# Mixer's room in two pools, the first down pair's weights beside the output projection, pinned forms in the second pass, loads in turns

## The chip, the cores and the metric

The kernel runs on 1 core of one Trainium2 chip. The metric is the device time of one execution in microseconds, taken as the median of several runs. The profile comes from one execution of its own.

## The reference, cut to what matters

Two layers of a decoder trunk on x of 256 rows and 2048 columns, all in float32:

```
for l in range(2):
    h    = rmsnorm(x, attn_norm_g[l])
    proj = h @ w_in[l]                    # 2048 x 6144: q | k | v | gate_b | gate_c | conv_in
    attn = diff_attention(norm(q), norm(k), v)     # 8 heads, T5 bias, difference of two softmaxes
    conv = gate_b * causal_conv3(gate_c * conv_in)
    x    = x + concat([rmsnorm(attn) * c, conv]) @ w_out[l]     # 2048 x 2048
    x    = x + relu(rmsnorm(x) @ w_up[l])**2 @ w_down[l]        # 2048 x 8192 x 2048
```

## The kernel before, in words

**Products.** Every float32 product is made of three products of rounded parts (TERMS): each operand is split into a high part, rounded by ACT, and a low part, the remainder, made by DVE. So each weight tile costs one load (issued on SP's queue), one ACT operation (`whi`, `uhi`, `b1h` and the like) and one DVE operation (`wlo`, `ulo`, `b1l`). The class Weights holds such jobs in a list; `take()` gives the next one to the matmuls and makes up to three more ahead (AHEAD).

**Order.** PE's instructions run in the order in which they are traced. For the other engines, a scheduler with a simulated timeline chooses the order at compile time; an engine then runs its list strictly in that order. The helper `late` pins an instruction behind the one traced before it on its engine. `Background` pieces are generators; `work.tick()`, called between matmuls, moves each of them on, so transpositions, norms and attention are laid between the matmuls of the projections.

**Mixer.** x stands in four chunks of 512 columns. At the start `first_loads` loads x and the first weights, and `Norm.chunk` transposes a chunk on PE (eight 128x128 pieces, `tpn`), splits it with the gain (`split_gained`, ACT L255 and DVE L256) and squares it for the norm (ACT L437). The squares are pinned. Chunk 0's loads alternate with the halves of the first weight (`cut`). Thirteen small tensors (gains, taps, lambdas, the bias table) are loaded on POOL's queue. Then `linear` makes q, k and v of four heads, again for the other four, then the conv's parts (`gc`, `ci`, `gb`), then the output projection `o`, four columns of 22 us. Biases, q, k, v, conv and the concatenated result share one pool, `bpool`, with eight buffers of 8 KB a partition.

**MLP, first pass.** The hidden width is cut into 32 blocks of 256. For block i, PE makes two columns of the up product (`up`, `upw`, `upc`, L856), ACT and DVE evict, apply ReLU (L873), scale (L875) and square (L877), and `rounded` splits the result into f (L893, L894), stored to DRAM by POOL (`plain`, `hid`). Two blocks behind it (LAG), 30 of the blocks multiply with w_down's left half by a Strassen-like scheme of seven products (L902) in place of eight. Its weight forms are made by `quarters`: `b1`, `b2` from the raw rows (`draw`), `t13` and `t24` from sums `t` (L754, L757, L758), each split by L740 (ACT) and L741 (DVE). One such set is called a pair here. `b2`, `t` and `t13` have one buffer, `b1` and `t24` two, `draw` three. The first pair is made by `begin`, called after block 0's square, and pinned. The last two blocks (30 and 31) multiply plainly (L982).

**MLP, second pass.** For w_down's right half the blocks come back: the plain ones from `plain` in pairs called `block(b)` (`g`, loaded on POOL's queue), 24 matmuls each (L1061); the twelve in SEVEN = 4, 6, 8, 11, ... from `hid` with the seven products (21 matmuls, L902, `rt`). `made_in` orders where the weights are made: `slots` lays the four jobs of a SEVEN block (plain, sums, its f, more) between those of the plain blocks before it.

**Pools.** Pools are laid one after another and a later pool waits for the tiles that lie under it. In the MLP `upool` (24 KB) and `fpool` (24 KB) lie under `dpool` (24 KB) and `spool` (48 KB).

Of the kernel before, what the change touches and what calls it, by code (L numbers as in the profile page):

```python
# [9 lines left out]
F32 = mybir.dt.float32  # L10
# [92 lines left out]
def trunk(ctx: ExitStack, tc: tile.TileContext, x, w_in, w_out, conv_w, q_norm_g, k_norm_g,  # L103
# [30 lines left out]
    def load_x(n, lo=0, hi=CH):  # L134
        nc.sync.dma_start(
            xs[n][:, :, lo:hi],
            x[0, :, n * CH + lo:n * CH + hi].rearrange("(t p) c -> p t c", p=P))
# [6 lines left out]
    nc.vector.memset(ones, 1.0)  # L144
    warm = bank("warm")
# [16 lines left out]
    ngains = const.tile([P, NG], F32, tag="ngains", name="ngains")  # L162
# [12 lines left out]
    nc.gpsimd.dma_start(vec[0:NCW, :], conv_w.rearrange("l i (k p) -> (l i k) p", p=P))  # L175
    for i, g in enumerate((q_norm_g, k_norm_g)):
        for m in range(2):
            nc.gpsimd.dma_start(
                vec[QG + i * DEPTH:QG + (i + 1) * DEPTH, m * DK:(m + 1) * DK], g)
    nc.gpsimd.dma_start(vec[QG + 2 * DEPTH:MG, :], subln_g)  # L180
    nc.gpsimd.dma_start(vec[MG:ROWS, :], mlp_norm_g.rearrange("l (k p) -> (l k) p", p=P))
    lamv = const.tile([1, 4, DEPTH, DK], F32, tag="lamv", name="lamv")
    for i, a in enumerate((lambda_q1, lambda_q2, lambda_k1, lambda_k2)):
        nc.gpsimd.dma_start(lamv[:, i], a[None])
    sel = const.tile([NB + 1, REL], F32, tag="sel", name="sel")
    nc.gpsimd.dma_start(sel, selector)
    rel = const.tile([NB + 1, 2 * NH], F32, tag="rel", name="rel")
    nc.vector.memset(rel[NB:NB + 1, :], NEG)
    nc.gpsimd.dma_start(rel[0:NB, :], rel_bias)
# [44 lines left out]
    def load_bias(l, bpool, bias):  # L234

        if l == 0:
            yield from small_setup()
        revs = []
        for j in range(2):
            rev = bpool.tile([P, NH, S], F32, tag="b", name=f"rev{l}{j}")  # L240
# [12 lines left out]
    def split_gained(dst, k, src, gain):  # L253

        nc.scalar.activation(dst[:, 0, k], src, AF.Copy, scale=gain)  # L255
        nc.vector.scalar_tensor_tensor(  # L256
            dst[:, 1, k], src, gain, dst[:, 0, k].bitcast(F32), op0=ALU.mult, op1=ALU.subtract)
# [15 lines left out]
    class Weights:  # L273
# [9 lines left out]
        def halves(self, raw, c=slice(None)):  # L283

            i = len(self.made)
            shape = [P] + list(raw.shape[1:])
            hi = wpool.tile(shape, F32R, tag="hi", name="whi")
            lo = wpool.tile(shape, F32R, tag="lo", name="wlo")
            first = self.cut and i < 2
            for k in (slice(0, 1), slice(1, None)) if first else (slice(None),):  # L290
                a = nc.scalar.activation(hi[:, k], raw[:, k], AF.Copy)  # L291
                d = nc.vector.tensor_sub(lo[:, k], raw[:, k], hi[:, k].bitcast(F32))  # L292
                if first:
                    late(a)
                    late(d)
            return hi, lo

        cut = False

        def plain(self, w, row, c, nk):  # L300
# [7 lines left out]
            def load():  # L308
                raw = self.pool.tile([P, nk, cols], F32, tag="raw", name="raw", bufs=RAW)
                src = w[row:row + nk * P, c:c + cols].rearrange("(k p) c -> p k c", p=P)  # L310
                if self.cut and not self.made and not self.early:
                    for k in range(nk):
                        load_x(0, k * CH // 2, (k + 1) * CH // 2)
                        nc.sync.dma_start(raw[:, k], src[:, k])
                else:
                    nc.sync.dma_start(raw, src)
# [10 lines left out]
        def take(self):  # L327
# [4 lines left out]
            ahead = min(max(i - 1, 0), AHEAD) if self.cut else AHEAD  # L332
# [5 lines left out]
            return self.made.pop(i) if not self.cut else self.made[i]  # L338
# [69 lines left out]
    class Norm:  # L408
# [3 lines left out]
        def __init__(self, which, l):  # L412
            self.which, self.l = which, l
            self.tiles = [Parts(apool, "a", f"nT{which}{l}_{n}") for n in range(D // CH)]
            self.ss = small.tile([P, NT, D // CH], F32, tag="ss", name=f"ss{which}{l}", bufs=2)

        def chunk(self, n, wait, banks=None):
            yield wait
            a = self.tiles[n].open()
            for j in range(2):  # L420
# [12 lines left out]
                if j == 0 and n == 0 and (self.which, self.l) == (0, 0):  # L433
                    yield 1
# [6 lines left out]

        def factors(self):
            while not all(t.ready == KG for t in self.tiles):
                yield 1
# [179 lines left out]
    def mixer(l, norm, loads):  # L624

        with ExitStack() as scope:
# [3 lines left out]
            bpool = scope.enter_context(tc.tile_pool(name="bpool", bufs=8))  # L630
            weights = Weights(rpool)
            weights.cut = l == 0
# [13 lines left out]
            work.start(load_bias(l, bpool, bias), 10)  # L646
            hT = norm.tiles
            cat = [Parts(bpool, "b", f"cat{l}{i}") for i in range(4)]
            work.start(norm.factors(), 1)
            for half in range(2):  # L650
# [3 lines left out]
                qT = bpool.tile([P, 2, 4, S], F32R, tag="b", name=f"qT{l}{half}")  # L654
                work.start(qk_norm(acc, r, qT, q_gain[:, l:l + 1], f"q{l}{half}"))
                acc = linear(f"k{l}{half}", hT, weights)
                kT = bpool.tile([P, 2, 4, S], F32R, tag="b", name=f"kT{l}{half}")
                work.start(qk_norm(acc, r, kT, k_gain[:, l:l + 1], f"k{l}{half}"))
                acc = linear(f"v{l}{half}", hT, weights)
                v = bpool.tile([P, 2, NT, CH], F32R, tag="b", name=f"v{l}{half}")  # L660
# [7 lines left out]
            cv = bpool.tile([P, AW // P, S], F32, tag="b", name=f"cv{l}")  # L668
# [24 lines left out]
    def mlp(l, mnorm, last):  # L693
# [3 lines left out]
        with ExitStack() as scope:  # L697
            upool = scope.enter_context(tc.tile_pool(name="upool", bufs=3))
            fpool = scope.enter_context(tc.tile_pool(name="fpool", bufs=2))
            dpool = scope.enter_context(tc.tile_pool(name="dpool", bufs=3))  # L700
            spool = scope.enter_context(tc.tile_pool(name="spool", bufs=1))
# [22 lines left out]
            def load_rows(i, col):  # L724
                raw = (upool.tile([P, 2, 2 * CH], F32, tag="uraw", name="raw") if col and i not in SEVEN else
                       dpool.tile([P, 2, 2 * CH], F32, tag="draw", name="draw"))
# [5 lines left out]
            def quarters(i, col=0):  # L732


                keep = late if i == 0 and col == 0 else lambda ins: None

                def parts(src, tag, bufs):
                    hi = spool.tile(list(src.shape), F32R, tag=f"{tag}h", name=f"{tag}h", bufs=bufs)
                    lo = spool.tile(list(src.shape), F32R, tag=f"{tag}l", name=f"{tag}l", bufs=bufs)
# [10 lines left out]
                def sums():  # L750
                    raw = forms["raw"]
                    t = forms["t"] = spool.tile([P, 4, CH], F32, tag="t", name="t")
# [51 lines left out]
            def load_again(i):  # L804
                again[i] = fpool.tile([P, 8, P], F32, tag="h", name="h", bufs=2)
# [24 lines left out]
            for i in SEVEN:  # L830
                before = [j for j in mine if j < where[i]][-4:]
# [37 lines left out]
            def square(i, h):  # L869
# [18 lines left out]
                nc.gpsimd.dma_start(plain[b // 2][:, b % 2], f[:, :, :4])  # L888
# [8 lines left out]
            prods = {}  # L897
# [8 lines left out]
            for i in range(NP):  # L906
                j = i - LAG
                end = i == NP - 1
                h = fpool.tile([P, 8, P], F32, tag="h", name="h", bufs=2)
                if i == 0:  # L910
# [8 lines left out]
                    forms["begin"]()  # L919
# [85 lines left out]
            for i in range(NP):  # L1005
# [29 lines left out]
                if slot == 0 and b == 0:  # L1035
                    block(1)
# [33 lines left out]
    def first_loads(weights):  # L1070
        for n in range(1, D // CH):
            weights.load_early(2)
            load_x(n)
            work.start(norm.chunk(n, 2), 4 * n - 2)
        work.start(norm.chunk(0, 0))
        work.tick()
        warm_up(5)
# [36 lines left out]
```

## Time and profile before

| what | us |
|---|---|
| median of 3 runs | 2163.86 (2161.31 to 2164.84) |
| the profiled execution | 2163.51 |
| its span, first to last instruction | 2161.7 |
| mean granted TensorE clock | 0.996 |
| DVE busy | 1692.1 |
| ACT busy | 1301.1 |

Times in rows are microseconds from the start of the span. In a row of the waits stand the engine and line, what it waited for, then the total, the number of times and the longest. In a row of the timeline stand start, duration, engine, line, operation, tiles, shapes and count, and in brackets the idle time before it with what ended that. In a row of the chain of waits stand start, duration and what. In a row of a window stand its two ends, its length, the busy time and instruction count of PE, PEld, DVE, ACT and POOL, then the granted clock, the DMA share and GB/s. In a row of the groups, "x84 | 102.4, 1219" is the count, the busy time in us and the mean in ns.

### The profile page before, as it was taken

The numbers are of one execution on the slowest core, as the hardware profiler recorded it, in microseconds if no ns is written. First come the engines' busy times: TensorE is split into PE (matmuls) and PEld (weight loads), VectorE is DVE, ScalarE is ACT, GpSimd is POOL, SyncE is SP. The second block draws the span as 40 slices with busy tenths as digits, with TensorE's granted clock in tenths as the row PEclk, the third lists the DMA queues.
The fourth block names the chain that finished last, engine by engine and source line by source line (L and its number), as shares of the span: only waits on it lengthen the run. The fifth ranks groups of instructions, "written<-read, shape, count | busy, mean of one in ns | idle before, by whom it ended". The sixth has DMA issues, their size and how long they took to land.

```text
span 2161.7 us, 29004 instructions
## 1 busy us (share of the span) xinstructions
PE 2136.9 (99%) x10966; PEld 1815.0 (84%) x10966; DVE 1692.1 (78%) x2301; ACT 1301.1 (60%) x1760; POOL 176.1 (8%) x266
## 2 busy tenths in 40 slices
PE   9999999999999999999999999999999999998999
PEld 7888888788888888788888888888888888887887
DVE  5677655699888888889766776557988888887796
ACT  6556445576666667556565654446766666665563
POOL 3021200000000000100001222000000000001000
PEclk9999999999999999999999999999999999999999
DMA  7555766587777777888456557656877777779882
GB/s 256 177 165 162 240 186 189 175 260 237 230 229 226 231 233 229 298 302 301 165 171 180 159 165 244 186 165 217 259 231 225 231 234 225 227 231 304 308 299 77
DMA packets 288413, 477.05 MB, mean 221 GB/s; under 512 B 10931, under 2 KB 191749, under 8 KB 288272
## 3 DMA queue, kind: packets, MB, share of 16 engines
q1 hardware_dynamic: 268128, 417.89, 61.8%
q0 software_dynamic: 20096, 57.28, 7.8%
q8 instruction: 86, 1.41, 0.3%
q14 instruction: 55, 0.45, 0.1%
q10 hardware_dynamic: 48, 0.02, 0.0%
HBM read 441.04 MB, written 34.10 MB: 220 GB/s over the span
## 4 chain that ended last, share of the span: by engine, by line
PE 92%; DVE 3%; DMA 2%; issue 2%; POOL 1%; ACT 1%; DVEq 0%; POOLq 0%; ACTq 0%
PE upc L856 30%; PE pr L902 13%; PE rt L1061 10%; PE o L361 8%; PE rt L902 5%; PE ci L383 4%; PE gc L383 4%; PE gb L383 4%; PE v L361 4%; PE q L361 3%; PE k L361 3%; DMA draw<-in_w_down_dram 1%; PE up L856 1%; PE pr L982 1%; DVE ulo L720 1%
## 5 line engine op out<-in xcount | busy, mean ns | idle before, releaser
L292 DVE TENSOR_TENSOR wlo<-raw,whi 128x1024 fp32r<-128x1024 f32 (+1 forms) x338 | 414.6, 1229 | 273.7 <-ACT whi L291 267.8
L291 ACT ACTIVATE whi<-raw 128x1024 fp32r<-128x1024 f32 (+1 forms) x338 | 356.0, 1055 | 437.6 <-PE rt L1061 120.5
L856 PE MATMUL upc<-nT,uhi 128*128 128x512 f32 x1920 | 477.6, 391 | 0.0
L719 ACT ACTIVATE uhi<-uraw 128x1024 fp32r<-128x1024 f32 x256 | 270.4, 1056 | 262.8 <-PE upc L856 228.0
L856 PEld LDWEIGHTS upc<-nT,uhi 128*128 128x128 f32 x1920 | 352.7, 188 | 68.3
L720 DVE TENSOR_TENSOR ulo<-uraw,uhi 128x1024 fp32r<-128x1024 f32 x256 | 313.0, 1223 | 115.2 <-ACT uhi L719 104.8
L856 PEld LDWEIGHTS upc<-nT,ulo 128*128 128x128 f32 x1920 | 261.9, 190 | 18.7
L856 PE MATMUL upc<-nT,ulo 128*128 128x256 f32 x1920 | 267.7, 282 | 0.0
L1061 PE MATMUL rt<-whi,g 128*128 128x512 f32 x608 | 191.9, 389 | 0.0
L361 PE MATMUL o<-whi,cat 128*128 128x512 f32 x512 | 159.6, 390 | 0.0
L1061 PEld LDWEIGHTS rt<-whi,g 128*128 128x128 f32 x608 | 114.1, 188 | 23.6
L1061 PE MATMUL rt<-wlo,g 128*128 128x512 f32 x304 | 118.3, 389 | 0.0
L361 PEld LDWEIGHTS o<-whi,cat 128*128 128x128 f32 x512 | 96.1, 188 | 19.8
L741 DVE TENSOR_TENSOR t13l<-t,t13h 128x1024 fp32r<-128x1024 f32 x84 | 102.8, 1223 | 3.1
L741 DVE TENSOR_TENSOR b2l<-draw,b2h 128x1024 fp32r<-128x1024 f32 x84 | 102.3, 1218 | 1.1 <-ACT b2h L740 1.1
L754 DVE TENSOR_TENSOR t<-draw 128x1024 f32<-128x1024 f32 x84 | 102.3, 1218 | 0.6 <-DMA draw<-in_w_down_dram 0.6
L741 DVE TENSOR_TENSOR t24l<-t,t24h 128x1024 fp32r<-128x1024 f32 x84 | 102.4, 1219 | 0.2
L361 PE MATMUL o<-wlo,cat 128*128 128x512 f32 x256 | 99.6, 389 | 0.0
L894 DVE TENSOR_TENSOR f<-h,f 128x896 fp32r<-128x896 f32 (+2 forms) x88 | 98.7, 1121 | 0.2
L902 PE MATMUL pr<-t13h,f 128*128 128x512 f32 x240 | 93.8, 391 | 0.0
L740 ACT ACTIVATE t13h<-t 128x1024 fp32r<-128x1024 f32 x84 | 89.4, 1064 | 6.4 <-PE rt L902 2.4
L740 ACT ACTIVATE b2h<-draw 128x1024 fp32r<-128x1024 f32 x84 | 88.4, 1052 | 6.4 <-PE pr L902 3.8
(359 smaller groups left out, 3831.9 us busy)
## 6 DMA issues: line engine op xcount, KB each, us to landing
uraw<-in_w_up_dram SPq DMA_DIRECT2D x128, 1024.0 KB, 5.9
raw<-in_w_in_dram SPq DMA_DIRECT2D x191, 512.0 KB, 4.0
draw<-in_w_down_dram SPq DMA_DIRECT2D x88, 1024.0 KB, 5.9
raw<-in_w_down_dram SPq DMA_DIRECT2D x40, 1024.0 KB, 6.4
raw<-in_w_out_dram SPq DMA_DIRECT2D x64, 512.0 KB, 3.7
plain<-f POOLq DMA_DIRECT2D x40, 512.0 KB, 3.8
g<-plain POOLq DMA_DIRECT2D x40, 512.0 KB, 9.6
hid<-h POOLq DMA_DIRECT2D x24, 448.0 KB, 6.1
```

The costliest lines, as they stand in the source:

```text
L291: a = nc.scalar.activation(hi[:, k], raw[:, k], AF.Copy)
L292: d = nc.vector.tensor_sub(lo[:, k], raw[:, k], hi[:, k].bitcast(F32))
L361: nc.tensor.matmul(acc[:, t], a.ap[:, pa, k % KG, t * P:(t + 1) * P], (hi, lo)[pw][:, j], start=(k == 0 and n == 0), stop=(k == nk - 1 and ...
L383: nc.tensor.matmul(acc[:, f, 0] if part else acc[:, f], wt[:, k % 4, fs], a.ap[:, 0, k % KG] if part else a.ap[:, :, k % KG], start=(part ...
L719: nc.scalar.activation(hi, src, AF.Copy)
L720: nc.vector.tensor_sub(lo, src, hi.bitcast(F32))
L740: keep(nc.scalar.activation(hi, src, AF.Copy))
L741: keep(nc.vector.tensor_sub(lo, src, hi.bitcast(F32)))
L754: keep(nc.vector.tensor_sub(t[:, 0:2], raw[:, :, 1], raw[:, 0]))
L856: nc.tensor.matmul(acc[:, 0] if part else acc, wt[:, k], a.ap[:, 0, k % KG] if part else a.ap[:, :, k % KG], start=(part == 0 and kh == 0 ...
L902: nc.tensor.matmul(prods[n], f[:, pa, a], b[pw], start=(start and m == 0), stop=(stop and m == 2))
L1061: nc.tensor.matmul(prods[p], blocks[b][:, slot, pa, 2 * k + t], w[pw][:, n], start=(i == PLAIN[0] and k == 0 and m == 0), stop=False)
```

## The change

Five edits:

- The start. `Norm.begin` replaces the chunks of the first norm: eight steps, each of four transpositions and then, in turn for two columns k, the split of x (ACT, DVE) and half a weight (ACT, DVE), all pinned. The squares come in behind the sixth step and later. x's first half chunk is the first load, the second half goes on ACT's queue; a one-column copy on ACT comes early; the small loads move from POOL's queue to SP's, pinned behind the loads of x; three warm-up matmuls stand where five stood.
- The mixer's pool of eight buffers becomes two pools of four single-buffer tags: `cats` (the four concatenated tiles, and before them q, k, v of the first half) and `spare` (bias tables, q, k, v of the second half, conv).
- In the MLP `second` and `first` replace `dpool` and `spool`; `tile_of` gives each tile its room by turns. `upool` (24 KB), `fpool` (20 KB), `second` (32 KB), `first` (44 KB): `second` lies on the room of `cats`, `first` on that of `spare`. The first pair is made entirely where the jobs are listed, ahead of the up product in the trace, and is not pinned.
- In the second pass the forms of the first SEVEN block (4) are pinned, and its jobs stand behind weights 0, 1, 5 and 3 instead of 4 to 7.
- `block(1)` is issued on POOL behind the last store of `plain`.

```diff
+    load_x(0, 0, CH // 2)
     nc.scalar.dma_start(ngv, attn_norm_g.rearrange("l (k p) -> (l k) p", p=P))
+    load_x(0, CH // 2, CH, nc.scalar)
+    nc.scalar.activation(ngains[:, :1], ones[:, :1], AF.Copy)
...
+    def small_loads():
+        def load(dst, src):
+            late(nc.sync.dma_start(dst, src))
...
+        def in_turns(self, split):
+            j = self.traced
+            self.traced += 1
+            raw = self.early.pop(0) if self.early else self.jobs[j].load()
+            hi, lo = self.made[j] = self.pair(raw)
+            for k in range(2):
+                split(k)
+                late(nc.scalar.activation(hi[:, k], raw[:, k], AF.Copy))
+                late(nc.vector.tensor_sub(lo[:, k], raw[:, k], hi[:, k].bitcast(F32)))
...
+        def begin(self, weights):
+            at = 0
+            for j, step in enumerate((0, 1, 3, 4, 6, 8, 10, 12)):
+                if step > at:
+                    yield step - at
+                    at = step
...
+                if j == 0:
+                    warm_up(3)
+                weights.in_turns(lambda i: split_gained(...))
+                if j >= 5:
+                    self.squares(j - 5)
+            yield 1
+            self.squares(3)
...
-            bpool = scope.enter_context(tc.tile_pool(name="bpool", bufs=8))
+            cats = scope.enter_context(tc.tile_pool(name="cats", bufs=1))
+            spare = scope.enter_context(tc.tile_pool(name="spare", bufs=1))
...
-            dpool = scope.enter_context(tc.tile_pool(name="dpool", bufs=3))
-            spool = scope.enter_context(tc.tile_pool(name="spool", bufs=1))
+            second = scope.enter_context(tc.tile_pool(name="second", bufs=1))
+            first = scope.enter_context(tc.tile_pool(name="first", bufs=1))
+            def tile_of(tag, shape, dtype, *rooms):
+                n = turn[tag] = turn.get(tag, -1) + 1
+                pool, tag_in = rooms[max(n - (tag == "draw"), 0) % len(rooms)]
+                return pool.tile(shape, dtype, tag=tag_in, name=tag, bufs=1)
...
-                keep = late if i == 0 and col == 0 else lambda ins: None
+                keep = late if i == SEVEN[0] and col else lambda ins: None
...
                 if i == 0 and col == 0:
-                    made = {}
-                    begin = lambda: made.update(p=plain(), s=sums())
-                    forms["begin"] = begin
-                    return lambda: made["p"], lambda: made["s"], more
+                    made = [plain(), sums(), more()]
+                    return tuple(lambda n=n: made[n] for n in range(3))
...
-                before = [j for j in mine if j < where[i]][-4:]
+                before = [j for j in mine if j < where[i]][-4:] if i != SEVEN[0] else [
+                    mine[0], mine[1], mine[5], mine[3]]
...
-                nc.gpsimd.dma_start(plain[b // 2][:, b % 2], f[:, :, :4])
+                stored.append(nc.gpsimd.dma_start(plain[b // 2][:, b % 2], f[:, :, :4]))
...
-                    block(1)
+                    with tc.issue_after(stored[-1].ins):
+                        block(1)
```

More of the change, by code (lines that the diff above doesn't have):

```diff
@@ L283, in halves, with pair @@
         def halves(self, raw, c=slice(None)):
-            i = len(self.made)
-            shape = [P] + list(raw.shape[1:])
[L287 to L298, printed above, removed]
+            hi, lo = self.pair(raw)
+            nc.scalar.activation(hi, raw, AF.Copy)
+            nc.vector.tensor_sub(lo, raw, hi.bitcast(F32))
+            return hi, lo
+        def pair(self, raw):
+            shape = [P] + list(raw.shape[1:])
+            return (wpool.tile(shape, F32R, tag="hi", name="whi"),
+                    wpool.tile(shape, F32R, tag="lo", name="wlo"))
+        turns = 0
+        def in_turns(self, split):
[7 more added lines that the diff above has]
+                late(nc.vector.tensor_sub(lo[:, k], raw[:, k], hi[:, k].bitcast(F32)))
         def plain(self, w, row, c, nk):
@@ L310, in load @@
                 src = w[row:row + nk * P, c:c + cols].rearrange("(k p) c -> p k c", p=P)
-                if self.cut and not self.made and not self.early:
+                if row < KG * P and self.turns and not self.used:
                     for k in range(nk):
-                        load_x(0, k * CH // 2, (k + 1) * CH // 2)
                         nc.sync.dma_start(raw[:, k], src[:, k])
@@ L337, in take @@
                 self.made[j] = self.jobs[j]()
-            return self.made.pop(i) if not self.cut else self.made[i]
+            return self.made.pop(i)
         def straight(self, w, row0, nk, col):
@@ L1073, in first_loads @@
             load_x(n)
[L1074 to L1077, printed above, removed]
+        small_loads()
+        work.start(norm.begin(weights))
     for l in range(DEPTH):
```

98 lines of the change are left out of this document (59 added, 39 removed).

## The prediction

> **What bounds the kernel now.** I read the page first, then the chain of waits for PE, then the timeline and the busy time by window around every place where PE stood.
>
> ```profile
> PE   2136.9 (99%) x10966; PEld 1815.0 (84%) x10966; DVE 1692.1 (78%) x2301; ACT 1301.1 (60%) x1760; POOL 176.1 (8%) x266
> ...
> PE pr L982 <- ACT f L893: 5.4, 2, 3.9
> PE pr L902 <- DVE t13l L741: 4.0, 2, 2.4
> PE pr L982 <- DVE f L894: 4.0, 2, 2.3
> PE q L361 <- ACT whi L291: 2.3, 2, 1.9
> PE up L856 <- DVE nT L256: 1.5, 2, 0.8
> ```
>
> PE is busy for 2136.9 of 2161.7 us. The change neither adds nor removes a matmul of the network, so all it can win is PE's idle time and the time that PE runs slowly after idling. The rows show that idle time in three places: L982 (the end of the first pass of each MLP, 9.4 us over both layers), L902 with t13l (the first down pair of each layer, 4.0 us), and the start. The change touches each of these three. I cost them one at a time, with a full-speed matmul taken from the chain of waits below: 14.99 us for 66, so 0.227 us each.
>
> **Start.** Columns of the first rows: start, duration, what; of the window row: busy time of PE, PEld, DVE, ACT, POOL, then granted clock.
>
> ```profile
> 4.10 1.28 ACT L255 ACT_TABLE_LOAD   x1 [4.10 <-DVE ngains L163]
> ...
> 7.47 0.50 PE L361 MATMUL q<-whi,nT 128*128 128x512 f32 x1 [0.39 <-ACT whi L291]
> ...
> 12.73 3.03 ACT L291 ACTIVATE whi<-raw 128x512 fp32r<-128x512 f32 x4
> ...
> 13.40 0.62 PE L361 MATMUL q<-whi,nT 128*128 128x512 f32 x1 [1.93 <-ACT whi L291]
> ...
> 7.47:39.63 32.16, 29.47 (x131) 22.45 (x132) 20.98 (x41) 21.45 (x43) 5.34 (x8) 0.95 0.77 252
> ...
> 40.01 14.99 PE k L361 x66
> ...
> 2.69 0.43 SPq L316 DMA_DIRECT2D raw<-in_w_in_dram  x1
> ```
>
> The first product starts at 7.47. Then PE waits until 13.40, because ACT finishes both splits of chunk 0 and its two squares before it starts the second weight at 12.73. In the q stage PE idles 32.16 - 29.47 = 2.7 us, and a clock of 0.95 costs 0.05 x 32.16 = 1.6 us more. The new order (one split, one half weight, in turn) puts the first half weight behind one split instead of two, and moves the table load at 4.10 under the DMA wait: about 1.2 us off 7.47. The squares move behind the sixth transposition, so the 13.40 wait goes. Together 1.2 + 2.7 + 1.6 = 5.5 us. What is late next is the low half: a half split and a half weight on DVE stand between a transposition and its product, and I leave 0.7 us for that. Term: -4.8 us.
>
> Edits around it. The thirteen small loads leave POOL for SP; at 0.43 us an issue that is 5.6 us of SP. They are pinned behind the last x load, which is ready early, and the fifth weight cannot be issued before the first is split, so they fill a stretch in which SP waits: nothing, at most 3 us if the fifth weight queues behind them all. POOL makes the identity sooner. The ACT queue takes half of x0: two issues, ahead of anything ACT can compute. Two warm-ups fewer and the gains' dummy copy: nothing.
>
> **First down pair.** Window row, then the DVE form that is repeated:
>
> ```profile
> 306.00:395.00 89.00, 89.00 (x406) 73.93 (x406) 49.14 (x53) 42.62 (x58) 0.00 (x0) 1.00 0.54 160
> ...
> L741 DVE TENSOR_TENSOR t24l<-t,t24h 128x1024 fp32r<-128x1024 f32 x84 | 102.4, 1219 | 0.2
> ```
>
> The first pair's raw rows can be loaded only when the mixer's whole pool is free, so its forms are made after the output projection, in a stretch where PE then waits for t13l. With two pools the forms' room lies on the tiles that the gate frees before the projection. One pair costs DVE four operations of 1.22 us and three half-size ones, some 7 us. In the projection DVE is busy 49.14 and ACT 42.62 of 89 us and the DMA share is 0.54: cover for 7 us of DVE, 4 us of ACT and a 1 MB load several times over. Weights are made three ahead there, so a form that waits some us for its load on DVE does not reach PE. Term: -4.0 us. The L856 wait of 1.5 us comes from the normalised x and stays. The rooms by turns instead of by free slot are the same number of buffers: nothing, from -1 to +3 us (two t13l waits of 1.7 to 2.4 show the size of a miss).
>
> **End of the first pass.** The timeline (the first matmul after the last of up, then ACT), the chain of waits, the windows from the stop of PE to its last matmul of L982 in each layer, and ACT's row of layer 1:
>
> ```profile
> 899.27 0.40 PE L902 MATMUL pr<-t13h,f 128*128 128x512 f32 x1
> ...
> 904.23 0.63 ACT L740 ACTIVATE b1h<-draw 128x512 fp32r<-128x512 f32 x1 [2.42 <-DMA draw<-in_w_down_dram]
> 904.77 0.61 ACT L873 ACTIVATE h<-h 128x512 f32<-128x512 f32 x1
> ...
> 895.58 8.62 DMA draw<-in_w_down_dram
> ...
> 908.95 0.68 DVE t L757
> ...
> 906.94:918.27 11.33, 7.58 (x26) 5.83 (x26) 10.02 (x13) 5.17 (x6) 0.72 (x1) 0.85 1.12 408
> 1976.94:1991.98 15.04, 9.38 (x26) 7.01 (x26) 11.78 (x15) 6.95 (x9) 0.71 (x1) 0.66 1.03 353
> ...
> 1976.63 0.63 ACT L740 ACTIVATE b1h<-draw 128x512 fp32r<-128x512 f32 x1 [4.83 <-DMA draw<-in_w_down_dram]
> ```
>
> The ReLU of the last hidden block (L873) stands on ACT behind b1h, a form of the second pass whose load lands late (8.62 us). So f, the last operand of the first pass, is late, PE stops, and afterwards it runs at a granted 0.85 and 0.66. The last block needs 24 matmuls, 5.45 us; the windows are 11.33 and 15.04 us. So the two ends cost 5.9 and 9.6 us. With the first forms of the second pass pinned behind the block's own work, nothing that waits for a load stands before L873. From the last up matmul at 899.3 the chain has seven steps (eviction, sum, ReLU, ratio, square, two roundings) of at most 0.7 us, as the rows of 0.61 and 0.68 for such tiles show: some 5 us. f is first needed at 906.9: it fits. Block 1's loads, now behind the last store on POOL, leave the transfers free that b1h's load was fighting; the store comes sooner too, and block 1 is needed two blocks (48 matmuls, 11 us) after the end of L982, so its cost is nothing. Of 15.5 us I take 14.5.
>
> The clock is the one place where a rule weighs on the size. The rows give a clock of 0.85 and 0.66 in windows with idle stretches of 1.5 to 3.9 us. The Trainium skill, "TensorE: Matmul & The Clock Gate", section "HAM oscillation — how this bites in real kernels", asks only that idle gaps stay under about 3.4 us. By that rule all but the longest gap would have cost just its own length, and the removal would be worth 9.4 us here, not 15.5. This trace does not agree, since the clock fell after gaps of 1.5 (5.4 less 3.9) and 2.3 us in layer 0.
>
> What pays for it: the pinned forms leave a slack stretch for the start of the second pass.
>
> ```profile
> 895.00:918.00 23.00, 19.25 (x85) 15.44 (x84) 17.02 (x21) 11.52 (x14) 5.02 (x9) 0.93 1.10 394
> 912.00:934.00 22.00, 22.00 (x93) 18.04 (x92) 17.46 (x20) 9.33 (x9) 1.46 (x3) 0.94 0.88 327
> 934.00:944.00 10.00, 10.00 (x46) 8.29 (x45) 5.30 (x6) 5.30 (x6) 1.06 (x2) 1.00 0.84 289
> 944.00:955.00 11.00, 11.00 (x50) 9.13 (x49) 9.95 (x11) 7.07 (x8) 0.00 (x0) 1.00 0.92 331
> ```
>
> DVE idles 6.0 us, 4.5 us and 4.7 us in the first three windows and 1.1 us in the fourth. Into the first three go the 7 us of forms, and 5.9 us vanish with PE's stop: 12.9 of about 13 us (the windows overlap by 6 us, in which DVE hardly idles). So DVE comes to its dense stretch (9.95 of 11) with no reserve. From nothing to 2 us a layer; I take 0.5 each, +1.0 us.
>
> **Sum.** -4.8 - 4.0 - 14.5 + 1.0 = -22.3 us against the profiled execution's 2163.51 us: 2141.2. The median shown is 0.35 us higher than that execution, so I say 2141.
>
> **Rivals.**
> 1. The stop moves, not goes (0.20). Only the first pair of the second pass is pinned. The form at 904.23 may belong to a later pair, since two pairs are prepared ahead, and can still be put ahead of the square or the rounding. For it: rows show b1h ordered before a ReLU that is older in the program. Against: its load is issued later now, so an order by expected landing puts it later. PE then keeps, say, 10 of the 15.5 us: 2151.
> 2. DVE becomes the bound in the second pass (0.10). Seven units then wait a little for t13l or f. For it: 9.95 of 11 us. Against: no wait of PE in that stretch now. At 1 us in half of the 24 units it takes 12 us: 2153.
> 3. Slower (0.07). The same mechanism with no recovery: DVE's backlog never clears, and every one of the 24 units makes PE wait. It decides from 1.1 us a unit (27 us beyond the gain); at 1.3 us and with the clock falling after each: 2172.
> 4. The start does not gain (within the others): the small loads on SP hold up the fifth weight and PE idles at the ninth product instead: 2146.
>
> By the clock rule alone, 6 us less gain, it would be 2147; I give that 0.02.
>
> **How the numbers follow.** My forecast has 0.61 and its own range is 2136 to 2147: the lower end has every loss removed including the L856 waits and no new one, the upper end a missed start. With rivals 1 and 2 the range is 2136 to 2156; outside remain rival 3 and the worst of rival 2. A measurement can tell about 0.2%, 4.3 us, from no change. Faster 0.88: the forecast, rival 1, the clock case and nearly all of rival 2; within 0.2% 0.05, where rivals 1 and 2 come together; slower 0.07.
>
> **What would show it.** Right: the first q product near 6.2 us and no wait near 13 us, k starting near 35; DVE's first forms between 306 and 395 and no L902 wait for t13l; L873 directly after the eviction, L982 without a wait, a clock of 1.00 there. Wrong: an ACT row before L873 or L877 that waits for draw; L902 waits for t13l in the second pass; SP's small loads ahead of a weight that PE then waits for.

## The result and the profile after

The changed kernel takes 2152.01 us (median of 5 runs, 2150.66 to 2154.68) against 2163.86 (5 runs, 2161.06 to 2168.59): ratio 0.9948, 95% interval 0.9931 to 0.9964. It is faster by 11.9 us, where 22.9 were forecast. Its profiled execution took 2154.06 us, with a span of 2152.2 and a mean granted clock of 0.999.

The busy line of its page, first, and the chain of waits for PE:

```profile
PE 2133.2 (99%) x10962; PEld 1812.2 (84%) x10962; DVE 1691.1 (79%) x2307; ACT 1299.1 (60%) x1767; POOL 167.7 (8%) x253
```

```profile
PE tpn L444 <- DVE x L736: 3.4, 4, 1.5
PE o L379 <- DVE wlo L295: 3.2, 2, 1.6
PE up L915 <- DVE nT L264: 2.1, 2, 1.0
PE ci L401 <- ACT whi L294: 1.4, 2, 0.9
...
PE rt L1120 <- DVE wlo L295: 1.0, 3, 0.7
```

All the waits on which the prediction rested are gone: no product of the first pass waits for t13l or for f. In their place stand two waits that before did not have, both in the output projection (o, tpn), and a small one at conv_in (ci).

To see what each stretch is worth, I take the start of the same matmul in both profiles; the growth of the difference over a stretch is what it lost (+) or gained (-). For example, the first k product starts at 39.66 before and at 35.06 after: -4.60. Of this, 1.0 us is only the place of a product (`rbc`) that stands ahead of k before and among k's products after; from 48 us on, with `rbc` behind both, the difference is -3.6, and the table has that. Read from other matmuls, a step comes out up to 0.4 us different (the second pass of layer 0, for one, at 0.6 in place of 0.3).

| stretch | layer 0 | layer 1 | both | forecast |
|---|---|---|---|---|
| start, up to the k products | -3.6 | | -3.6 | -4.8 |
| conv_in | +0.7 | +1.3 | +2.0 | 0 |
| output projection, with the first up product | +4.7 | +6.4 | +11.1 | 0 |
| first down pair (t13l, t24l) | -3.0 | -2.4 | -5.4 | -4.0 |
| end of the first pass | -5.9 | -9.7 | -15.6 | -14.5 |
| second pass | +0.3 | +1.5 | +1.8 | +1.0 |
| sum | | | -9.7 | -22.3 |

All four terms of the prediction came out within 1.5 us. What is missing was lost beside them: 2.0 us at conv_in, where PE's wait varies from 0 to 1.9 us over the kernels below, and 11.1 us in a stretch that the prediction called covered. The start, by the timeline of PE and ACT in the changed kernel (start, duration, what, idle time before it and its releaser):

```profile
6.77 0.80 PE L379 MATMUL q<-whi,nT 128*128 128x512 f32 x1
...
35.06 0.39 PE L379 MATMUL k<-whi,nT 128*128 128x512 f32 x1
...
1.71 1.28 ACT L148 ACT_TABLE_LOAD   x1 [1.71 <-PEq L1155]
```

The window of its q stage, with the columns of the prediction's window rows:

```profile
6.77:35.04 28.27, 27.88 (x130) 21.44 (x130) 20.66 (x44) 20.98 (x48) 2.48 (x3) 1.00 0.80 260
```

The table load lies at 1.71 instead of 4.10, PE idles 28.27 - 27.88 = 0.4 us in the q stage and its clock is 1.00. The end of the first pass, by the timeline of ACT in layer 0:

```profile
898.15 0.58 ACT L925 ACTIVATE ev<-upc 128x512 f32<-128x512 f32 x1
...
900.11 0.62 ACT L932 ACTIVATE h<-h 128x512 f32<-128x512 f32 x1
901.36 0.63 ACT L936 ACTIVATE h<-h 128x512 f32<-128x512 f32 x1 [0.63 <-DVE h L934]
902.03 0.63 ACT L952 ACTIVATE f<-h 128x512 fp32r<-128x512 f32 x1
902.92 1.06 ACT L294 ACTIVATE whi<-draw 128x1024 fp32r<-128x1024 f32 x1 [0.26 <-PE pr L1040]
903.89 0.61 ACT L800 ACTIVATE b1h<-draw 128x512 fp32r<-128x512 f32 x1
```

And a window of that place in each layer:

```profile
900.00:910.00 10.00, 10.00 (x46) 8.28 (x45) 8.75 (x12) 7.90 (x11) 3.91 (x7) 1.00 0.76 226
1974.00:1982.00 8.00, 8.00 (x37) 6.60 (x36) 7.11 (x8) 5.75 (x8) 3.87 (x7) 1.00 0.86 243
```

The form b1h that stood before the ReLU now stands behind the last rounding f, and PE is busy for the whole of both windows at clock 1.00. Now the projection, by the timeline of layer 0, with rows of SP's queue, ACT, DVE and PE:

```profile
306.15 0.37 SPq L786 DMA_DIRECT2D draw<-in_w_down_dram  x1
...
314.17 0.63 ACT L800 ACTIVATE b1h<-draw 128x512 fp32r<-128x512 f32 x1 [4.23 <-DMA draw<-in_w_down_dram]
...
315.66 1.04 ACT L294 ACTIVATE whi<-raw 128x1024 fp32r<-128x1024 f32 x1
...
314.11 1.23 DVE L814 TENSOR_TENSOR t<-draw 128x1024 f32<-128x1024 f32 x1 [2.92 <-DMA draw<-in_w_down_dram]
...
317.60 1.22 DVE L295 TENSOR_TENSOR wlo<-raw,whi 128x1024 fp32r<-128x1024 f32 x1
...
318.87 0.50 PE L379 MATMUL o<-wlo,cat 128*128 128x512 f32 x1 [1.62 <-DVE wlo L295]
...
320.58 0.37 SPq L786 DMA_DIRECT2D draw<-in_w_down_dram  x1
...
327.83 1.23 DVE L814 TENSOR_TENSOR t<-draw 128x1024 f32<-128x1024 f32 x1 [2.74 <-DMA draw<-in_w_down_dram]
...
329.18 1.06 ACT L294 ACTIVATE whi<-raw 128x1024 fp32r<-128x1024 f32 x1 [3.56 <-DMA raw<-in_w_out_dram]
...
331.45 0.33 PE L444 MATMUL tpn<-ident,x 128*128 128x128 f32 x1 [1.49 <-DVE x L736]
```

And the window row that answers to the one the prediction quoted for this stretch:

```profile
306.00:395.00 89.00, 85.63 (x387) 70.18 (x386) 54.41 (x60) 44.18 (x60) 0.00 (x0) 1.00 0.56 177
```

Read it downwards. The load goes out at 306.15 and lands 8 us later, at 314.1. In the lists of ACT and DVE its forms stand in front of the next weight of the projection, so both engines stand still (4.23 and 2.92 us) though that weight could be made (in e2 below, ACT makes it at 311.58 and not at 315.66). After the landing DVE first makes t, b1l, b2l and another t; the weight's low half comes at 317.60, and PE has waited 1.62 us. The same happens again with the second pair's load at 320.58, which also sits in front of weight loads in SP's queue: DVE waits 2.74 us for the pair, ACT 3.56 us for a weight, and the sum x that PE transposes is late. PE idles 3.4 of 89 us; DVE is busy 54.41 and ACT 44.18, still far from full. It was never the amount of work.

Idle time explains 6.6 us (the rows tpn and o above) of the 11.1, and the longer wait of the first up product for nT another 0.6 (2.1 us against 1.5). In layer 1 the granted clock was 0.83 for ten us behind the second stop, which costs some 0.17 x 10 = 1.7 us:

```profile
1400.00:1410.00 10.00, 9.82 (x40) 8.34 (x41) 6.56 (x10) 5.55 (x11) 0.00 (x0) 0.83 0.51 169
```

I have not split the remaining 2.2 us further.

### The profile page after: what moved, and what is told of

It is laid out like the page before. It is cut to its first block, busy times and chain, and to the rows that moved or that the text cites. A ratio compares the mean times of both kernels' runs of the same rounds, so it can differ in the third digit from the quotient of the medians.

```text
span 2152.2 us, 28985 instructions
## 1 busy us (share of the span) xinstructions
PE 2133.2 (99%) x10962; PEld 1812.2 (84%) x10962; DVE 1691.1 (79%) x2307; ACT 1299.1 (60%) x1767; POOL 167.7 (8%) x253
## 4 chain that ended last, share of the span: by engine, by line
PE 90%; DVE 5%; DMA 3%; ACT 1%; issue 1%; POOL 0%; SPq 0%; DVEq 0%; ACTq 0%
PE upc L915 31%; PE pr L961 13%; PE rt L1120 8%; PE o L379 6%; PE rt L961 5%; PE v L379 4%; PE gb L401 4%; PE ci L401 4%; PE q L379 4%; PE gc L401 3%; PE k L379 3%; DMA draw<-in_w_down_dram 1%; DVE wlo L295 1%; DMA raw<-in_w_in_dram 1%; PE upw L915 1%; PE up L915 1%
## 5 line engine op out<-in xcount | busy, mean ns | idle before, releaser
L295 DVE TENSOR_TENSOR wlo<-raw,whi 128x1024 fp32r<-128x1024 f32 x328 | 404.4, 1236 | 242.3 <-ACT whi L294 237.0
L294 ACT ACTIVATE whi<-raw 128x1024 fp32r<-128x1024 f32 x328 | 346.4, 1059 | 404.1 <-PE rt L1120 86.3
L800 ACT ACTIVATE t24h<-t 128x1024 fp32r<-128x1024 f32 x84 | 88.4, 1052 | 22.2 <-DVE t L818 22.2
```

The costliest lines, as they stand in the source:

```text
L294: nc.scalar.activation(hi, raw, AF.Copy)
L295: nc.vector.tensor_sub(lo, raw, hi.bitcast(F32))
L800: keep(nc.scalar.activation(hi, src, AF.Copy))
```

## The experiments

Theory: the loss is an order. Forms that wait for their own load were put in front of the projection's weights, on engines that run their lists strictly in turn. Rivals: the load itself disturbs the projection; the shifted start does; DVE's extra work does. Further, each of the other parts was made alone. Ratios are to the kernel before, with 95% intervals; 4 to 11 runs each. Before ran beside each set, with medians from 2161.0 to 2164.4, so across the sets the ratios compare better than the times.

| run | what | us | ratio |
|---|---|---|---|
| after | all parts | 2152.01 | 0.9948 [0.9931, 0.9964] |
| e1 | after, first pair's forms back behind block 0's square | 2141.59 | 0.9907 [0.9893, 0.992] |
| e2 | after, the forms ordered behind the 13th and 27th weight | 2142.07 | 0.9907 [0.9893, 0.992] |
| e9 | e1 without the line that asks for the load early | 2141.59 | 0.9897 [0.9883, 0.991] |
| e12 | e9, the load held back into the burst | 2144.64 | 0.9912 [0.9898, 0.9926] |
| e3 | before + start | 2160.22 | 0.9993 [0.9983, 1.0002] |
| e4 | before + pins, slots, later block 1 | 2149.67 | 0.9948 [0.9934, 0.9962] |
| e5 | before + pins | 2152.85 | 0.9945 [0.9932, 0.9957] |
| e6 | before + slots | 2161.98 | 0.9991 [0.9982, 1.0] |
| e7 | before + later block 1 | 2164.69 | 1.0003 [0.9993, 1.0012] |
| e8 | before + pins and slots | 2149.57 | 0.993 [0.9917, 0.9942] |
| e10 | before + rooms, forms beside the projection | 2162.59 | 0.9995 [0.9986, 1.0004] |
| e11 | before + rooms, forms at their old place | 2151.76 | 0.9944 [0.9931, 0.9958] |
| e13 | before, two rooms for draw instead of three | 2156.92 | 0.9968 [0.9956, 0.998] |

**e1 and e2: the same work at another place.** e1 keeps everything, but the first pair's forms are pinned where before had them.

```diff
-                    made = [plain(), sums(), more()]
+                    early.append(load_rows(0, 0))
...
+                    forms["begin"] = lambda: made.update(p=plain(), s=sums())   # called behind square(0, h)
```

> The changed kernel, but only the LOAD of the first down pair stays beside the output projection; its forms (ACT and DVE) are pinned behind the first hidden block's square again, as in the kernel before. Theory A (in the projection ACT and DVE stand in order behind forms whose load has not landed): the waits of the projection (steps of +4.7 us in layer 0 and +6.4 us in layer 1 against the kernel before) go, the waits for t13l and t24l (3.0 and 2.4 us) come back: about 2152 - 11.1 + 5.4 = 2146 us. Rival B (the 1 MB loads themselves delay the weights of the projection): the steps stay at half or more and the t13l waits come on top: 2152 to 2157 us.

e2 keeps the forms beside the projection, but tells the scheduler to put the first pair's behind the projection's 13th weight and the second pair's behind its 27th.

```diff
-                    made = [plain(), sums(), more()]
+                    made = behind(12, lambda: [plain(), sums(), more()])
...
+                if i == 1 and col == 0:
+                    return tuple(lambda f=f: behind(26, f) for f in (plain, sums, more))
```

> The changed kernel, with the first pair's forms ordered on ACT and DVE behind the 13th weight of the output projection and the second pair's behind its 27th, so that both loads have landed; loads where the scheduler puts them. Theory A: the projection loses nothing, t13l does not wait either: 2152 - 11.1 = 2141 us. Rival B (loads in the way): 2147 us or more. Rival C (ACT and DVE lack the capacity there): new waits for wlo at the new place, 2147 us or more.

The same window of the projection in e1, and then the chain of waits for PE in e2, longest rows first:

```profile
306.00:395.00 89.00, 89.00 (x411) 74.02 (x410) 49.58 (x54) 43.85 (x62) 0.00 (x0) 1.00 0.55 169
```

```profile
PE up L924 <- DVE nT L264: 2.1, 2, 1.0
PE q L380 <- DVE wlo L316: 1.3, 3, 0.9
```

In e1 PE is busy 89.00 of 89 us, although the pair's load goes out at the same place (305.62): the load alone does no harm. In e2 load and forms lie beside the projection and no wait for o or tpn is left: the forms' work alone does no harm either. So the order is shown to be the cause of the first stop, and both versions give back some 10 us (9 by the ratios): they beat both kernels. For the second stop e2 says less, because the second pair's load also moved, from 320.58 to 340.20, and e1 has no second pair there:

```profile
340.20 0.37 SPq L788 DMA_DIRECT2D draw<-in_w_down_dram  x1
```

Whether that stop, about half of the loss, came from forms in front of weights or from the load in front of weight loads is not separated.

What I had not expected is that e1 did not get the t13l wait back. It was to be 2146, and it is 2141.6. The forms beside the projection, then, are not what removed that wait. Two theories: the early load did, or the rooms did.

**e9, e12 and e13: what took the wait for t13l away.** e9 is e1 without the early request.

```diff
-                    early.append(load_rows(0, 0))
```

> The kernel with the first pair's load beside the projection and its forms pinned behind block 0's square (2141.6 us), with the one difference that the load is no longer asked for beside the projection: it is issued where the forms are. New start, rooms, pins, slots and later load of block 1 stay. Theory A (the early load alone takes the waits for t13l away): they come back, 2.5 + 0.5 us in the first layer and 1.9 + 0.5 in the second, 2145 to 2148 us. Theory B (the rooms in two pools free the load's place sooner, or the start's shift does it): no waits, 2141 to 2143 us.

It did not do its edit: SP's timeline shows the load at the same place, since the scheduler sends a load as soon as its room is free, and the room (`first`) is free by then.

```profile
305.86 0.37 SPq L786 DMA_DIRECT2D draw<-in_w_down_dram  x1
```

So e9 tells nothing apart between the theories; only that the explicit request is idle. What it led to is SP's queue at the beginning of the MLP. First before, with ACT's row for the up weight behind it; then e9:

```profile
395.57 0.37 SPq L712 DMA_DIRECT2D uraw<-in_w_up_dram  x1
396.11 2.79 SPq L727 DMA_DIRECT2D draw<-in_w_down_dram  x3
...
417.07 1.06 ACT L719 ACTIVATE uhi<-uraw 128x1024 fp32r<-128x1024 f32 x1 [4.46 <-DMA uraw<-in_w_up_dram]
```

```profile
392.87 1.23 SPq L786 DMA_DIRECT2D draw<-in_w_down_dram  x2
...
414.59 1.06 ACT L777 ACTIVATE uhi<-uraw 128x1024 fp32r<-128x1024 f32 x1 [1.69 <-DMA uraw<-in_w_up_dram]
```

Before has three free rooms, so three loads of 1 MB stand in a burst ahead of the next up weight, and ACT waits 4.46 us for that weight. With the new rooms one pair has been loaded already and two are in the burst. e12 puts the third load back into the burst with everything else new; e13 takes one out with everything else old.

```diff
+                    if i == 0 and not col:
+                        with tc.issue_after(ups[3].ins):     # the fourth load of the up weights
+                            raw = load_rows(i, col)
```

> The kernel of e9_no_early_load, where the first pair's load still went out beside the projection at 305.86 us, now with that load held behind the fourth load of the up weights, so that it goes out with the other two loads for block-of-seven weights in one burst of 3 MB at about 392 us, as in the kernel before. Theory A (a burst of three 1 MB loads ahead of the up weights' own load makes that load late, and ACT, DVE and the product for t13l with it): the waits come back, 2.5 + 0.5 us in the first layer and 1.9 + 0.5 in the second, 2145 to 2148 us against 2141.6. Theory B (the load's place has nothing to do with it; the rooms or the order of the forms took the wait away): 2141 to 2143 us, no wait.

```diff
-            dpool = scope.enter_context(tc.tile_pool(name="dpool", bufs=3))
+            dpool = scope.enter_context(tc.tile_pool(name="dpool", bufs=2))
```

> The kernel before with two rooms in place of three for the 1 MB loads of the down weights, and nothing else: the burst at about 396 us has two loads in place of three. Theory A (the burst's third load makes the wait): in both layers the product for t13l starts about 2 us sooner against its neighbours, 4 to 5.5 us in all; the second pass, which has a room less, loses part or all of it again by waits of its own, 2157 to 2166 us; the place in the first pass decides, not the total. Theory B: the wait at t13l is as before, 2.4 to 2.5 us in the first layer and 1.8 in the second.

The timeline of e12 with SP's burst and ACT's row for the up weight:

```profile
393.64 3.16 SPq L787 DMA_DIRECT2D draw<-in_w_down_dram  x3
...
413.01 1.06 ACT L778 ACTIVATE uhi<-uraw 128x1024 fp32r<-128x1024 f32 x1 [2.77 <-DMA uraw<-in_w_up_dram]
```

The wait of PE for t13l in e12:

```profile
PE pr L968 <- DVE t13l L802: 1.5, 2, 1.1
```

SP's burst in e13:

```profile
396.34 1.06 SPq L727 DMA_DIRECT2D draw<-in_w_down_dram  x2
```

And the three longest waits of PE in e13:

```profile
PE pr L982 <- DVE f L894: 6.8, 2, 3.6
PE q L361 <- ACT whi L291: 2.1, 2, 1.9
PE rt L1061 <- DVE wlo L292: 1.9, 2, 0.9
```

With the third load back the wait returns, at 1.5 us in place of 4.0; the steps at that product are +1.2 and +0.7 us against e9, and 2144.64 falls just short of theory A's 2145 to 2148. Of the 3.1 us between the two kernels, 0.7 already stand in the profiles ahead of the MLP. With one load fewer and nothing else, the wait is gone in both layers: steps of -2.5 - 0.3 and -1.8 - 0.5 us, 5.1 in all. Over all the profiles, each kernel with three loads in the burst has the wait (before and e3 to e8, 2.0 to 4.2 us; e12, 1.5), and each with two has none. In e3, though, only layer 0 has it: layer 1 sends three loads in a burst too and its t13l does not wait. The burst is shown to be the main cause, but three loads do not always make the wait; why, and why e12 has only 40% of it, is open. e13's total is 7 us under before's. In its profile the first pair is worth 5.1 us of that, a shorter stop at the end of the first pass (6.8 us for L982 instead of 9.4) another 5.0, and the second pass, with a room less, loses 3.0.

**e10 and e11: the rooms, with the forms beside the projection or not.** Both are before with the rooms in two pools and by turns; start and end of the first pass are as before.

```diff
-                    made = {}                              # e10 only
...
-                    forms["begin"] = begin
+                    made = [plain(), sums(), more()]
```

> The kernel before with the rooms in two pools and the first down pair's load and forms made beside the output projection as in the change; start and end of the first pass as before. Theory A (this step costs 4.7 + 6.4 us in the projection and gives 5.4 back): about 6 us slower than before, 2167 to 2172 us if before is 2161 to 2164. Theory B (the loss in the projection comes from the shifted start, not from these forms): 5 us faster, 2156 to 2159 us.

> The kernel before with the rooms in two pools and only the first down pair's load beside the output projection; its forms stay pinned behind block 0's square; start and end of the first pass as before. Theory A (the load alone is worth the 5.4 us of the t13l waits and costs the projection nothing): 2155 to 2159 us. Theory B (the load takes the place of a weight's load in the queue and the projection waits): 2160 to 2165 us.

The waits of e10, then of e11:

```profile
PE rt L1071 <- DVE wlo L292: 5.4, 7, 1.0
PE o L361 <- DVE wlo L292: 3.2, 2, 1.6
PE tpn L425 <- DVE x L689: 2.7, 4, 1.2
```

```profile
PE rt L1075 <- DVE wlo L292: 4.3, 6, 1.1
```

The pair is 10.8 us apart, and only in e10 do o and tpn wait: with the old start and without the pins the forms beside the projection cost 4.3 us in each layer there. That rules out the shifted start as the cause. Both totals were forecast too slow, by 7 and 5 us from the middle of theory A's range, because neither kernel waits at L982 any more, without any pin. e11's ACT shows the order that did it:

```profile
905.30 0.94 ACT L907 ACTIVATE f<-h 128x896 fp32r<-128x896 f32 x1
907.96 0.63 ACT L753 ACTIVATE b1h<-draw 128x512 fp32r<-128x512 f32 x1 [1.72 <-DMA draw<-in_w_down_dram]
```

With the new rooms and the earlier load, b1h stands behind f without being pinned. But DVE then waits for the same load in front of weights of the second pass, and rt waits for wlo: the second pass loses 3.9 and 1.7 us in e11, 4.2 and 2.9 in e10. So rooms and pins both remove the stop, which can be won only once, and with the pins and slots on top (e1) the waits in the second pass shrink too.

**e3 to e8: start, and end of the first pass, alone.** e3 is before with the new start, e4 before with pins, slots and the later block 1; e5 to e8 divide e4.

> The kernel before with the new start alone (loads in turns, small loads on SP). Theory: the start is worth what the matched matmuls show, 3.6 us after the k stage: 2160.3 us. Rival: part of the gain is lost again before the projection, by a shifted burst of loads in the conv stage: 2161.5 us.

> The kernel before with the three edits at the end of the first pass alone (pinned forms of block 4, its jobs earlier, block 1's loads behind the last store). Theory: the matched matmuls' gains of 5.9 and 9.7 us less 1.7 us of new waits in the second pass: about 2150 us (2148 to 2151). Rival: the gain needs the other edits too (another order of the scheduler): less than half of it, 2156 us or more. By the clock rule of the Trainium skill (idle gaps under about 3.4 us cost their length alone) the ends would be worth 9.4 us: 2156 us.

```diff
-                keep = late if i == 0 and col == 0 else lambda ins: None
+                keep = late if (i == 0 and col == 0) or (i == SEVEN[0] and col) else lambda ins: None   # e5: the pins
-                before = [j for j in mine if j < where[i]][-4:]
+                before = [j for j in mine if j < where[i]][-4:] if i != SEVEN[0] else [
+                    mine[0], mine[1], mine[5], mine[3]]                                                   # e6: the slots
-                    block(1)
+                    with tc.issue_after(stored[-1].ins):                                                  # e7: block 1 later
+                        block(1)
```

> The kernel before with one edit: the first forms of the second pass's first block of seven are kept where the text has them, behind the last block of the first pass. No slots, no later load. Theory A (the waits of 5.9 and 9.6 us at the end of the first pass come from ACT and DVE being queued behind the 1 MB load of those forms): the pin alone takes both waits away, -14 to -15.5 us, and the forms, now made late, cost the second pass 1 to 3 us a layer; about 2151 us against 2161 to 2164. Theory B (a pin without earlier slots only carries the wait into the second pass): the waits come back there as waits of products for the forms, 4 to 8 us a layer, and the time is 2157 to 2163.

> The kernel before with one edit: the slots at which the first block of seven's forms are made in the second pass move ahead; nothing is pinned and no load is later. Theory A: the forms are still hoisted in front of the last block's work, on the same load, so the waits at the end of the first pass stay: 2159 to 2165 us. Theory B (the place in the text sets the order): the gain of the three parts together, about 2150 us.

> The kernel before with one edit: the transfer of the second pass's block 1 is sent only behind the last store of the plain products' forms. Theory A (the forms wait for their own 1 MB load, which shares the DMA engines with block 1's three transfers): the load lands 1 to 4 us sooner and each of the two waits shrinks by that, 2156 to 2162 us; it cannot take them away. Theory B (the later transfer is only there to spare the second pass): no change at the end of the first pass, 2161 to 2165 us.

> The kernel before with the pin and the slots, without the later load of block 1. Theory A (pin and slots do the work): as with all three, 2149 to 2151 us. Theory B (block 1's transfer in front of the block of seven's load still delays it): products of the second pass wait 1 to 3 us more a layer, 2152 to 2156 us.

The waits of e5, then of e6, then of e7:

```profile
PE rt L1061 <- DVE wlo L292: 2.4, 4, 0.8
```

```profile
PE pr L983 <- ACT f L894: 5.6, 2, 3.4
PE pr L983 <- DVE f L895: 4.0, 2, 2.3
```

```profile
PE pr L982 <- DVE f L894: 4.5, 2, 2.3
PE pr L982 <- ACT f L893: 4.2, 2, 2.8
```

Theory A holds for e5, e6 and e8; e7 did what its theory B said. The pins alone remove both stops (-5.9 and -9.7 us at that place) and then wait 2.4 us more in the second pass. Slots alone or the later block 1 alone leave the stops at 9.6 and 8.7 us, against 9.4 before; their times cannot be told from before. With the slots on top of the pins the second pass's wait falls to 1.3 us (e8), and the later block 1 adds nothing that can be seen (e4 2149.67, e8 2149.57). So the three parts of e4 are worth what was worked out for that place, less the new waits.

In e3 the k products start 3.6 us earlier and keep it through v, but the total moves by 0.8 us, within what can be told from no change. Its 2160.22 is the theory's number only because that was worked out from 2163.86, and before took 2161.0 beside e3. conv_in gives 1.5 us back, where a weight stands in SP's queue behind a burst of three loads for the up product (ACT waits 8.43 us for it, before 6.82; PE then waits 1.4 us for whi). In the MLP of the profiled execution, layer 0 loses 1.4 us at the first down pair and 1.9 at the end of the first pass, and layer 1 wins 1.6 and 3.0 us at the same places, which the edit does not touch. So e3 says of the total only that it lies between 3.7 us less and 0.4 us more.

The profiles together say more of the start itself. Between 100 and 240 us, products stand on average 0.5 us ahead of before's in the nine profiles with the old start, before's own counted at 0 (from 0.2 behind to 1.1 ahead), and 3.3 us ahead in the six with the new one (2.5 to 3.6). So the start is worth some 2.8 us, and 3.6 was partly chance. The wait at conv_in does not go with it: it is 1.9 us in e7, with the old start, and 0.3 us in e9 and nothing in e12, with the new.

## Why the prediction was right and wrong

**The step that failed** is that of the first down pair: "cover for 7 us of DVE, 4 us of ACT and a 1 MB load several times over. Weights are made three ahead there, so a form that waits some us for its load on DVE does not reach PE." The measured idle shares were right, and they cannot answer the question. Cover is a matter of how long the engine is held at one place against how far ahead its weights are. ACT was held 4.23 us and then had two forms to make; DVE was held 2.92 us and had four, so the next weight's low half came 1.6 us too late. The prediction's own rows held the warning: a draw load took 8.62 us at the end of the first pass, and b1h stood there in front of an older ReLU. The same placing, in front of a load that lands late, was now new in the projection, and I saw it only where before already showed it. Cost: 11.1 us instead of nothing.

**The reason for that term's gain was wrong too.** The t13l waits did go, and were worth 5.4 rather than 4.0 us, but e1, e9 and e13 show that moving the forms had no part in it. "The rooms by turns instead of by free slot are the same number of buffers: nothing" was the second false step: which load has a room at which moment sets what SP sends, and that took away the burst's third load, and in e11 the stop at the end of the pass as well.

**The end of the first pass** came out as worked: 15.6 us for 14.5, the predicted order on ACT, clock 1.00 and nothing that waits for a load before the ReLU (L873 before, L932 after). The DVE slack that it counted as about 13 us is 13.9 by its windows (15.2 less the 1.3 us idle in their overlap); nothing hangs on that. The rivals "the stop moves" and "DVE becomes the bound" are out: no L982 wait is left in after, and the second pass lost 1.8 us for my 1.0. Which part did it is shown by e5 to e8: the pins; block 1's later transfer, which the prediction gave a share, has none.

On size, the row for 3.5 us of before's layer 0 behind its two stops of 1.49 and 2.26 us gives the clock (columns as in the other window rows):

```profile
911.50:915.00 3.50, 3.50 (x9) 2.78 (x10) 3.38 (x4) 1.06 (x1) 0.72 (x1) 0.54 1.14 411
```

The matmuls of the two windows therefore cost more than the 9.4 us of waits, and e4 and e5 win back 15 us there. The rule of the Trainium skill, "TensorE: Matmul & The Clock Gate", section "HAM oscillation — how this bites in real kernels", which asks only for gaps of under about 3.4 us, does not agree with this trace: in layer 0 stops of 1.49 and 2.26 us were followed by 0.54. Nor does every stop bring the clock down: in after's layer 0 the two main stops of the projection, 1.62 and 1.49 us, 12.6 us apart, left it at 1.00, and in layer 1 nearly the same pair, 1.61 and 1.42 us, 12.5 us apart, was followed by 0.83 over ten us. So the length of the stops and their distance do not decide alone; what does is open.

**The start** was right in its mechanism and too large: -3.6 for -4.8 in this pair of profiles, the first product at 6.77 where 6.2 was expected, and by all the profiles some 2.8 us. The 2.0 us at conv_in in after are not shown to come from it, since kernels with the old start wait there too. The range held the time; the likeliest value missed it by 11 us.

## What to carry to other kernels

On an engine that runs its list in order, spare busy time covers an added step only if its input has already landed; before moving work beside other work, compare its load's time from issue to landing with the lead of the work queued behind it, and order it behind enough of that work by hand. Count rooms as queue positions: each free buffer lets one more transfer go out ahead of something urgent, so one buffer fewer can be faster. And split a change of several parts before crediting its gain: here the version with one part undone is 9 to 10 us better than the whole, and two other parts each remove the same stop.

## What the runs showed that I had not expected

- A buffer count of 2 instead of 3 for the down weights' loads is worth 7 us (e13, ratio 0.9968 [0.9956, 0.998]).
- The median time from issue to landing of such a load in after is 6.3 us over the whole kernel; the two in layer 0's projection took 8.0 and 7.2 us.
- The same stop at the end of the first pass is removed by pinned forms (e5) and by a new rule for rooms (e11), with different waits left in the second pass: 2.4 and 4.3 us.
- The explicit early load of e1 and its absence in e9 are the same kernel to the chip: the load goes out at 305.62 and 305.86 us, and both medians are 2141.59.
